# Moving the past keys' norms of a hybrid encoder step into its S5 phase, with a changed formula for them

## The chip, the cores and the metric

One core of a Trainium2 chip runs the whole program. The metric is device microseconds (us) of one execution. The kernel before took 1456.39 us, the median of 3 runs (1454.52 to 1458.11).

## The reference

One step of a two-layer encoder, over 512 prompt tokens and 32 sample tokens that go through together (544 columns). Layer 0 has an S5 branch (a diagonal complex recurrence with a GLU gate) beside an attention into 256 memory tokens. Layer 1 has latent attention: a shared latent of 256 features gives the keys and values of 12 heads. The sample tokens also attend to 1024 cached positions, whose latents are an input. For these the keys have to be normed, head by head:

```python
m = rms_norm(mem[None], mem_norm_g[:, None, None, :])
kv = jnp.einsum('lbmd,ldk->lbmk', m, w_mem_kv)
...
latent_all = jnp.concatenate([past_latent.astype(new_latent.dtype), new_latent], axis=1)
...
k_nope = rms_norm((latent_all @ w_uk).reshape(Bsz, Lk, MLA_HEADS, NOPE_DIM), k_nope_norm_g)
```

The kernel needs only the sums of squares of those cached keys (64 features for each of 12 heads and 1024 positions); the scores themselves are taken with the query pulled through `w_uk`, and multiplied by the inverse norm afterwards. The two layers end in gated feed-forward blocks that take most of the time.

## The kernel before

Everything is float32 at almost full precision: an operand is split into a high part rounded to `float32r` and a low part, the rest, and a product takes three matmuls (high by high, high by low, low by high; `combos`). A weight is loaded twice: once plainly by SP's queue into `wraw`, from which ScalarE (ACT) writes the high part and the negated high part, and once by an accumulating transfer from GpSimd's (POOL's) queue, which adds the weight onto the negated high part and so leaves the low part (`weights`, L227 to L235). Everything else with a gain or a norm is split by ACT (high) and VectorE (DVE, low).

The program is written as stages and generators. A framework sorts the instructions of each engine beforehand, by the order of writing and by the table `ORDER`: a unit with a positive number is put earlier by so many places, one with a negative number later. At run time each engine, SP's and POOL's queues among them, works its list strictly in order, so an instruction that waits holds back all behind it. PSUM's eight banks and the pools of SBUF slots (`F`, `R`, `WR`, `WH`, `WL`) are taken and given back in the order of writing.

Two places matter here.

*The S5 phase* (67 to 174 us) has six steps `m`. A step transposes its inputs (`s5_input`), makes weights on DVE (`s5_wv`, `s5_wc`), writes a small kernel to DRAM and reads it back in another layout (the tile `kp` gets its diagonal added by POOL at L707, L710 writes it to `kd`, L719 reads it), scans on DVE (`s5_scan`, L752 to L780), multiplies out (`s5_output`, L791 and L792, transposes at L803) and applies GELU. Between the steps `fill` puts units of `mem_kv`: eight that project 256 memory rows by a quarter of the features of one layer (matmuls at L350; the rows are multiplied by the gain and split by ACT at L344 and DVE at L345), then nine that take norms, transposes and outputs. By `fills` seven of the first eight are written into steps 0 to 4, the eighth into step 5, and seven of the nine behind the last step. Then comes the memory attention of layer 0 (`mem_attend`, L430 to L520) and the GLU product (a GEMM like all others, matmuls at L324).

*The query phase* of layer 1 (742 to 866 us) has, in this order of writing: latents of the new tokens (L1197 to L1248), three groups of queries in turn, `q_front(g)` (a projection, L1289 and L1308) and `q_back(g)` (norm and rotation on DVE and POOL, L1298 to L1339, transposes at L1345 and L1351), beside them `key_norms`, then `absorb` (L1364 to L1375) and `sample_scores` (L1423). `key_norms` has three groups of four heads. For each it splits the group's part of `w_uk`, and for each of nine tiles of positions (eight of the past, 128 each, and one of 32 new ones) it multiplies six times (L1395: positions on the partitions, 256 columns), squares on ACT (L1399) and sums by head on DVE (L1401). `rsqrt` of the whole table `kss` follows. `load_past` loads the past latents and splits them; `sample_scores` needs them too.

Of the kernel before, what the change touches and what calls it, by code (L numbers as in the profile page):

```python
# [18 lines left out]
KD = D // 128  # L19
# [31 lines left out]
for _n, _w in (("mix", 2 * KD), ("bglu", NM), ("ffn", 2 * KD), ("kv", KD), ("mem", 2 * KD), ("ql", NM),  # L51
# [8 lines left out]
NCN = 468  # L60


ORDER = {"q_front": -50, "q_back": -20, "absorb": -100, "mem_kv": -60, "mem_kv_end": 580, "s5_scan": 400,
         "s5_input": 260, "norm0": 20, "s5_params": -50, "mem_attend0": 100, "s5_wc": 10, "q_front0": 10, "norm1": 0,
         "att1": 30, "att2": 20, "mem_attend1": 20, "load_past": -100, "queries": 10, "key_norms": 60,
         "latents": 1250, "queries2": -160}
# [71 lines left out]
def body(ctx, tc, A, O):  # L138
# [67 lines left out]
    def gcol(name, i):  # L206
        c = GP[name] + i
        return gp[:, c:c + 1]
# [125 lines left out]
    def mem_kv(fm, rm, bm, b1, dst):  # L334
        ps = [[bm.get(512) for _ in range(2)] for _ in range(2)]
        acc = fm.get(2, NMEM)
        for u in range(4):
            mt = fm.get(2, NMEM)
            nc.sync.dma_start(mt, A["mem"][:, 2 * u:2 * u + 2, :])
            for l in range(2):  # L340
                hi, lo = rm.get(2, NMEM), rm.get(2, NMEM)
                for k2 in range(2):
                    g = gcol("mem", l * KD + 2 * u + k2)
                    S.activation(hi[:, k2], mt[:, k2], AF.Copy, scale=g)  # L344
                    V.scalar_tensor_tensor(lo[:, k2], mt[:, k2], g, hi[:, k2].bitcast(F32), ALU.mult, ALU.subtract)  # L345
                w = weights(A["w_mkv"][l, u], 1024, lo_eng=V if l else P)
                for t in range(2):
                    for k2 in range(2):
                        for i, (x, ww) in enumerate(combos((hi, lo), w)):
                            T.matmul(ps[l][t], x[:, k2, 128 * t:128 * t + 128], ww[:, 512 * k2:512 * k2 + 512],  # L350
                                     start=u == 0 and k2 == 0 and i == 0, stop=u == 3 and k2 == 1 and i == 2)
                wfree(w)
                rm.put(hi, lo)
                if l:
                    if u:
                        q = fm.get(2, NMEM)
                        S.activation(q, mt, AF.Square)
                        P.tensor_tensor(acc, acc, q, ALU.add)
                        fm.put(q)
                    else:  # L360
                        S.activation(acc, mt, AF.Square)
                    fm.put(mt)
                yield
# [10 lines left out]
        for l in range(2):  # L374
            kt, v = dst[l]
            ss = sm(8, "mss")
            q = fm.get(2, 256)
            for t in range(2):
                S.activation(q[:, t], ps[l][t][:, :256], AF.Square, scale=r[:, t:t + 1])
                S.activation(v[:, t, :], ps[l][t][:, 256:], AF.Copy, scale=r[:, t:t + 1])  # L380
            V.tensor_reduce(ss, view(q, [[64, 8], [1, 64]]), AX.X, ALU.add)
            P.dma_start(O["mem_v"][l].rearrange("t p c -> p t c"), v)
            yield
            x = sm(8, "mkx")
            V.tensor_scalar(x, ss, 1.0 / 64, EPS, ALU.mult, ALU.add)
            y = rsqrt(x, 128, 8, "mkr")
            fm.put(q)
            V.tensor_tensor(y.rearrange("p (t h) -> p t h", t=2), y.rearrange("p (t h) -> p t h", t=2),
                            view(r, [[1, 2], [0, 4]]), ALU.mult)
            yield  # L390
            kk = fm.get(2, 256)
            for t in range(2):
                V.tensor_tensor(kk[:, t].rearrange("p (h d) -> p h d", d=64),
                                ps[l][t][:, :256].rearrange("p (h d) -> p h d", d=64),
                                view(y, [[1, 4], [0, 64]], 4 * t), ALU.mult)
            bm.put(*ps[l])
            kf = view(kk, [[64, 8], [1, 64]])
            V.tensor_tensor(kf, kf, view(grow(f"mk{l}"), [[0, 8], [1, 64]]), ALU.mult)
            P.dma_start(O["mem_k"][l].rearrange("t p c -> p t c"), kk)
            yield  # L400
            pt = b1.get(512)
            for hp in range(2):
                for t in range(2):
                    T.transpose(pt[:, 256 * hp + 128 * t:256 * hp + 128 * t + 128],
                                kk[:, t, 128 * hp:128 * hp + 128], ident)
            S.activation(kt.rearrange("p a b -> p (a b)"), pt, AF.Copy, scale=mqg[:, l:l + 1])
            b1.put(pt)
            fm.put(kk)
            yield

    def mem_cache(l, fm):
        kt, v, raw = fm.get(2, NMEM), fm.get(2, 256), fm.get(2, NMEM)
# [588 lines left out]
    exr.close()  # L1001
    exr = ExitStack()
    lr = exr.enter_context(tc.tile_pool(name="l0b", bufs=1, reuse_waits="tile"))
    R, fx = slots(lr, 4, F32R, 512, "rb"), slots(lr, 3, F32, FW, "fx")
    FA, FB, FD = slots(lr, 2, F32, 1024, "wv"), slots(lr, 1, F32, 2 * FW, "tb"), slots(lr, 3, F32, 2 * FW, "wc")
    fxs = list(fx.free)
    F.merge(fx)
# [1 line left out]
    kvp = F.get(2, NMEM), F.get(2, 256)  # L1009
    mkv = mem_kv(F, R, BG, BS, (kvp, (mk1, mv1)))  # L1010

    fills = ((1, 2, 1), (1, 1, 0), (1, 0, 0), (0, 1, 0), (1, 1, 0), (1, 1, 0), (7,))
    nfill = 0

    def fill(n):
        nonlocal nfill
        for _ in range(n):
            unit("mem_kv" if nfill < 8 else "mem_kv_end", mkv)
            nfill += 1
    wvs = []  # L1020

# [43 lines left out]
    while unit("s5_output_end", g_out) is not g_out:  # L1065
        pass
    fill(20)
    P.dma_start(O["ssm"], q5["hf"])
    F.retire(big, *fxs)
    exr.close()  # L1070
# [305 lines left out]


    def key_norms():
        ss = sm(108, "kss", 1)
        tc.keep_in_program_order(V.memset(ss, 1.0))  # L1380
        for g in range(3):
            raw, w = F.get(2, 256), (R.get(2, 256), R.get(2, 256))
            nc.sync.dma_start(raw, A["w_ukv"][g][:, :, :256])
            split(*w, raw)
            F.put(raw)
            for tp in range(5):
                b = BK.get(512)
                n = NS if tp == 4 else 128
                for j in range(1 if tp == 4 else 2):
                    t = 2 * tp + j  # L1390
                    for k in range(2):
                        x = lat[k] if tp == 4 else past[t // 4][k]
                        c0 = 512 if tp == 4 else 128 * (t % 4)
                        for c, (xx, ww) in enumerate(combos(x, w)):
                            T.matmul(b[:n, 256 * j:256 * j + 256], xx[:, c0:c0 + n], ww[:, k], start=k == 0 and c == 0,  # L1395
                                     stop=k == 1 and c == 2)
                q = F.get(512)
                m = 256 if tp == 4 else 512
                S.activation(q[:n, :m], b[:n, :m], AF.Square)  # L1399
                BK.put(b)  # L1400
                V.tensor_reduce(view(ss[:n], [[12, m // 256], [1, 4]], 24 * tp + 4 * g),  # L1401
                                q[:n, :m].rearrange("p (j h d) -> p j h d", h=4, d=64), AX.X, ALU.add)
                F.put(q)
                if tp % 2:
                    yield
            R.put(*w)
            yield
        x = sm(108, "kx", 1)
        V.tensor_scalar(x, ss, 1.0 / NOPE, EPS, ALU.mult, ALU.add)
        res["rk"] = rsqrt(x, 128, 108, "krs")  # L1410


# [388 lines left out]
```

## Time and profile before

| | us |
|---|---|
| median of 3 runs | 1456.39 |
| lowest, highest | 1454.52, 1458.11 |
| profiled execution, its own time | 1456.27 |
| its span, first to last instruction | 1454.5 |
| PE busy | 1407.3 (97%) |
| ACT busy | 754.4 (52%) |
| DVE busy | 721.8 (50%) |
| POOL busy | 358.5 (25%) |

The profiled execution lies 0.12 us from the median, and 1.8 us of it are outside the span. Busy shares are means over stages with different limits: the feed-forward blocks keep PE (TensorE) at work without a break, and only the S5 phase, the start and a few places in layer 1 show it idle. The page's line of the granted clock (PEclk, tenths of full speed) has a dip in the same places. A time read in the trace is counted from the span's start.

### The profile page before, as it was taken

What the parts mean: (1) busy time and instruction counts of PE and PEld (TensorE: products, weight loads), DVE (VectorE), ACT (ScalarE), POOL (GpSimd) and SP (SyncE); (2) the same over time, 40 slices, a digit from 0 to 9 for tenths busy, and PEclk for the clock granted to TensorE, in tenths of its full rate; (3) what the DMA queues carried; (4) which work ended last, traced back from release to release, by engine and by line L of the source; (5) the groups of instructions that cost most, each with busy time, mean ns of one, the idle gap of its engine ahead of it and who ended that gap; (6) DMA issues with size and microseconds to landing.
All of it is one profiled execution on the core that took longest, in us unless ns stands there. A gap on an engine that the chain in (4) does not pass through costs nothing.

```text
span 1454.5 us, 26917 instructions
## 1 busy us (share of the span) xinstructions
PE 1407.3 (97%) x10693; PEld 1314.2 (90%) x10693; DVE 721.8 (50%) x1810; ACT 754.4 (52%) x1247; POOL 358.5 (25%) x622
## 2 busy tenths in 40 slices
PE   8977799999999999999989999999999999999998
PEld 7966689999999999999988987557999999999998
DVE  7988742355513551455247755663355513551351
ACT  6655655555534553456554554654555534553452
POOL 2131232312211221124326422332322211221121
PEclk9989889999999999999999999999999999999999
DMA  8754627778878878869741432012778888878775
GB/s 264 167 139 111 165 59 176 164 173 176 177 173 175 175 174 175 175 143 205 151 124 58 108 112 54 19 30 52 160 174 177 172 176 175 179 170 179 172 159 138
DMA packets 71902, 214.77 MB, mean 148 GB/s; under 512 B 8128, under 2 KB 17312, under 8 KB 71776
## 3 DMA queue, kind: packets, MB, share of 16 engines
q0 software_dynamic: 27616, 96.16, 37.4%
q1 hardware_dynamic: 43008, 114.80, 27.4%
q10 hardware_dynamic: 1152, 2.10, 0.5%
q8 instruction: 84, 1.38, 0.4%
q14 instruction: 42, 0.34, 0.1%
HBM read 207.41 MB, written 5.61 MB: 146 GB/s over the span
## 4 chain that ended last, share of the span: by engine, by line
PE 86%; DVE 4%; DMA 4%; ACT 3%; issue 2%; POOL 1%; SPq 0%; DVEq 0%; POOLq 0%; ACTq 0%
PE bank L324 66%; PE bank L1308 2%; PE bank L1556 2%; PE bank L1395 2%; PE bank L1592 1%; DMA wlo<-i_w_in 1%; PE bank L1509 1%; PE bank L1483 1%; PE bank L1197 1%; DMA wlo<-i_w_f 1%; PE bank L350 1%; PE bank L1581 1%; PE bank L482 1%; PE bank L520 1%; PE bank L1423 1%
## 5 line engine op out<-in xcount | busy, mean ns | idle before, releaser
L324 PE MATMUL bank<-rc,whi 128*128 128x272 f32 x3728 | 628.3, 289 | 0.2 <-DVE rc L305 0.2
L324 PEld LDWEIGHTS bank<-rc,whi 128*128 128x128 f32 x3728 | 529.7, 189 | 5.2 <-issue 4.3
L324 PE MATMUL bank<-rc,wlo 128*128 128x272 f32 x1864 | 389.0, 289 | 0.8 <-DMA wlo<-i_w_in 0.8
L231 ACT ACTIVATE whi<-wraw 128x1024 fp32r<-128x1024 f32 (+2 forms) x186 | 191.2, 1028 | 361.0 <-issue 314.4
L324 PEld LDWEIGHTS bank<-rc,wlo 128*128 128x128 f32 x1864 | 293.7, 188 | 1.3 <-DMA wlo<-i_w_in 1.0
L324 PE MATMUL bank<-g,whi 128*128 128x272 f32 x1408 | 234.6, 288 | 0.7 <-ACT g L216 0.7
L324 PEld LDWEIGHTS bank<-g,whi 128*128 128x128 f32 x1408 | 198.8, 188 | 1.3 <-ACT g L216 1.2
L233 POOL DMA_DIRECT2D wlo<-i_w_f x136 | 117.4, 863 | 304.1 <-ACT wlo L232 302.2
L232 ACT ACTIVATE wlo<-wraw 128x1024 fp32r<-128x1024 f32 (+2 forms) x186 | 188.9, 1016 | 3.7 <-PE bank L350 3.1
L324 PE MATMUL bank<-g,wlo 128*128 128x272 f32 x704 | 145.9, 289 | 2.4 <-DMA wlo<-i_w_f 2.4
L851 DVE SCALAR_TENSOR_TENSOR fa<-fa,gp,fa 128x546 f32<-128x546 f32 x88 | 69.6, 791 | 139.7 <-ACT fa L850 139.7
L865 DVE TENSOR_TENSOR h<-bank,h 128x272 f32<-128x272 f32 x96 | 38.2, 435 | 173.0 <-PE bank L324 172.5
L324 PEld LDWEIGHTS bank<-g,wlo 128*128 128x128 f32 x704 | 110.4, 188 | 2.8 <-DMA wlo<-i_w_f 2.8
L850 ACT ACTIVATE fa<-fa,gp 128x546 f32<-128x546 f32 x88 | 73.1, 830 | 12.8 <-DVE fa L845 12.8
L843 DVE TENSOR_TENSOR fa<-bank,fa 128x272 f32<-128x272 f32 x88 | 38.9, 442 | 81.8 <-PE bank L324 77.6
L852 DVE SCALAR_TENSOR_TENSOR fa<-fa,gp,fa 128x546 f32<-128x546 f32 x88 | 69.6, 790 | 3.1
L891 ACT ACTIVATE fa<-fa 128x546 f32<-128x546 f32 x44 | 29.1, 662 | 71.8 <-DVE fa L852 71.8
L847 POOL COPY fa<-gp 128x2 f32<-128x2 f32 x88 | 20.9, 238 | 171.5 <-DVE g L217 108.0
L848 POOL COPY fa<-fa 128x4 f32<-128x4 f32 x88 | 18.0, 205 | 166.0 <-DVE fa L845 166.0
L324 PE MATMUL bank<-ra,whi 128*128 128x272 f32 x256 | 48.1, 311 | 2.3 <-ACT whi L241 2.3
L216 ACT ACTIVATE g<-fa 128x544 fp32r<-128x544 f32 x44 | 29.0, 658 | 37.6 <-DVE fa L893 37.6
L892 DVE TENSOR_TENSOR fa<-fa,fa 128x512 f32<-128x512 f32 x44 | 30.5, 693 | 33.5 <-ACT fa L891 33.5
(626 smaller groups left out, 1992.7 us busy)
## 6 DMA issues: line engine op xcount, KB each, us to landing
wraw<-i_w_f SPq DMA_DIRECT2D x120, 512.0 KB
wlo<-i_w_f POOLq DMA_DIRECT2D x120, 512.0 KB, 7.4
wraw<-i_w_out SPq DMA_DIRECT2D x16, 512.0 KB
wlo<-i_w_out POOLq DMA_DIRECT2D x16, 512.0 KB, 7.2
wraw<-i_w_in SPq DMA_DIRECT2D x14, 512.0 KB
wlo<-i_w_in POOLq DMA_DIRECT2D x14, 512.0 KB, 7.8
wraw<-i_w_f SPq DMA_DIRECT2D x16, 384.0 KB
wlo<-i_w_f POOLq DMA_DIRECT2D x16, 384.0 KB, 6.3
```

Of the source, the lines that this page charges most:

```text
L231: S.activation(hi, raw, AF.Copy)
L232: S.activation(lo, raw, AF.Copy, scale=-1.0)
L233: P.dma_start(lo, ap, accum_op=ALU.add)
L324: T.matmul(ps[q][:, :c], ww, xx[:, c0:c0 + c], start=k == 0 and i == 0, stop=k == n - 1 and i == 2)
L843: V.tensor_tensor(u[:, 2:274], ps[0][:, :272], rb[:, :272], ALU.mult)
L850: S.activation(y, u[:, 2:548], AF.Identity, scale=gcol("cw", 3 * ci + 2), bias=gcol("cb", ci))
L851: V.scalar_tensor_tensor(y, u[:, 1:547], gcol("cw", 3 * ci + 1), y, ALU.mult, ALU.add)
L852: V.scalar_tensor_tensor(y, u[:, 0:546], gcol("cw", 3 * ci), y, ALU.mult, ALU.add)
L865: V.tensor_tensor(h[m][:, c0:c0 + cc], ps[qd][:, :cc], h[m][:, c0:c0 + cc], ALU.add)
L891: S.activation(yg, yg, AF.Silu)
L892: V.tensor_tensor(u[:, 2:514], ya[:, :NP], yg[:, :NP], ALU.mult)
L1308: T.matmul(b[:, :384], xx[:, 128 * t:128 * t + 128], ww[:, 384 * (k % 2):384 * (k % 2) + 384], start=k == 0 and i == 0, stop=k == NM - 1 a ...
```

## The change

Three things change together.

1. The past keys' norms leave `key_norms` and become a generator `past_norms`, twelve units, put into the S5 steps. It works with features on the partitions: for each half of the positions (512) and each pair of heads, six matmuls of 512 columns with the weight as the stationary operand (L440), one square on ACT (L442), and four small float32 matmuls against `blk2` that sum 64 partitions each (L446) into a bank, which ACT copies into `kss` at the end of each half (L451). Latents and weights are loaded by SP's queue (L421, L430) and split as weights are: two ACT passes and an accumulating transfer from POOL's queue (L424, L433). The weights are loaded once for each half. `key_norms` keeps the 32 new positions alone. The past latents are still loaded and split in the query phase.
2. In `mem_kv` the multiplied rows are made by POOL (L343), the high and negated high part by ACT in passes of 512 columns, and the low part by an accumulating transfer from SBUF to SBUF (L346). DVE has no part in it.
3. `fills` puts all 17 units of `mem_kv` into steps 0 to 3, ten units of `past_norms` into steps 4 and 5 and two behind the last. `mem_kv_end` goes from 580 to 60. The pool `R` of the phase grows from 4 to 8 tiles, `fx` shrinks from 3 to 2.

```diff
-"mem_kv_end": 580
+"mem_kv_end": 60
...
             for l in range(2):
-                hi, lo = rm.get(2, NMEM), rm.get(2, NMEM)
+                hi, lo, gm = rm.get(2, NMEM), rm.get(2, NMEM), fm.get(2, NMEM)
                 for k2 in range(2):
-                    g = gcol("mem", l * KD + 2 * u + k2)
-                    S.activation(hi[:, k2], mt[:, k2], AF.Copy, scale=g)
-                    V.scalar_tensor_tensor(lo[:, k2], mt[:, k2], g, hi[:, k2].bitcast(F32), ALU.mult, ALU.subtract)
+                    P.tensor_scalar(gm[:, k2], mt[:, k2], gcol("mem", l * KD + 2 * u + k2), 0.0, ALU.mult, ALU.add)
+                S.activation(hi, gm, AF.Copy)
+                S.activation(lo, gm, AF.Copy, scale=-1.0)
+                P.dma_start(lo, gm, accum_op=ALU.add)
+                fm.put(gm)
...
+    def past_norms(fm, rm, bm, ss):
+        for hf_ in range(2):
+            c = slice(512 * hf_, 512 * hf_ + 512)
+            st = bm.get(512)
+            xs = []
+            for i in range(2):
+                raw, hi, lo = fm.get(512), rm.get(512), rm.get(512)
+                nc.sync.dma_start(raw, A["lat_past"][:, i, c])
+                S.activation(hi, raw, AF.Copy)
+                S.activation(lo, raw, AF.Copy, scale=-1.0)
+                P.dma_start(lo, A["lat_past"][:, i, c], accum_op=ALU.add)
+                fm.put(raw)
+                xs.append((hi, lo))
+            for g in range(3):
+                raw, wh, wl = fm.get(2, 256), rm.get(2, 256), rm.get(2, 256)
+                ap = A["w_ukv"][g][:, :, :256]
+                nc.sync.dma_start(raw, ap)
+                S.activation(wh, raw, AF.Copy)
+                S.activation(wl, raw, AF.Copy, scale=-1.0)
+                P.dma_start(wl, ap, accum_op=ALU.add)
+                fm.put(raw)
+                for j in range(2):
+                    b = bm.get(512)
+                    f = slice(128 * j, 128 * j + 128)
+                    for k in range(2):
+                        for i, (x, w) in enumerate(combos(xs[k], (wh[:, k, f], wl[:, k, f]))):
+                            T.matmul(b, w, x, start=k == 0 and i == 0, stop=k == 1 and i == 2)
+                    q = fm.get(512)
+                    S.activation(q, b, AF.Square)
+                    bm.put(b)
+                    for t in range(4):
+                        o = 12 * t + 4 * g + 2 * j
+                        T.matmul(st[:, o:o + 2], q[:, 128 * t:128 * t + 128], blk2, start=True, stop=True)
+                    fm.put(q)
+                    if j:
+                        rm.put(wh, wl)
+                    yield
+            S.activation(ss[:, 48 * hf_:48 * hf_ + 48], st[:, :48], AF.Copy)
...
-    fills = ((1, 2, 1), (1, 1, 0), (1, 0, 0), (0, 1, 0), (1, 1, 0), (1, 1, 0), (7,))
+    fills = ((2, 0, 0), (1, 1, 1), (1, 1, 1), (3, 4, 2), (2, 2, 1), (2, 2, 1), (2,))
...
     def key_norms():
...
-            for tp in range(5):
-                b = BK.get(512)
-                n = NS if tp == 4 else 128
...
+            b = BK.get(512)
+            for k in range(2):
+                for c, (xx, ww) in enumerate(combos(lat[k], w)):
+                    T.matmul(b[:NS, :256], xx[:, 512:512 + NS], ww[:, k], start=k == 0 and c == 0,
+                             stop=k == 1 and c == 2)
```

How the lists move is seen at three places. Line numbers are those of each kernel; the changed one has 44 lines more in front of the S5 helpers and some 50 in front of the query phase.

PE in the query phase, behind the second group's transposes (L1345 and L1351 before, L1395 and L1401 now). Before, `absorb` of groups 0 and 1 (L1364) is followed by 54 matmuls of `key_norms` (L1395; the first rows are shown):

```order
L1345 MATMUL bank_70<-cn,fa_91 96x128
L1351 MATMUL bank_63<-cn,fa_77 96x128
L1364 MATMUL bank_68<-qsT_6897,wraw_94 128x32 x8
L1364 MATMUL bank_64<-qsT_6898,wraw_95 128x32 x8
L1395 MATMUL bank_65<-rc_1895,rc_1885 128x256
```

Now, from the same point, absorb is L1414, and directly behind it stand the third group's 16 transposes (L1395), then its own absorb and the scores (L1463):

```order
L1395 MATMUL bank_70<-cn,fa_78 96x128
L1401 MATMUL bank_63<-cn,fa_86 96x128
L1414 MATMUL bank_68<-qsT_7083,wraw_94 128x32 x8
L1414 MATMUL bank_66<-qsT_7084,wraw_95 128x32 x8
L1395 MATMUL bank_64<-cn,fa_92 96x128
```

The 96 past matmuls of groups 1 and 2 that stood between the two sets of transposes, or among the second set, are gone, and nothing has taken their place.

PE between the last transposes of the S5 output (L803 before, L847 now) and the GLU product (L324). Before, the memory keys' transposes (L404) and the start of the memory attention (L430 to L482) stand there:

```order
L803 MATMUL bank_70<-cn,big 128x69 x4
L449 MATMUL bank_69<-fa_79,fa_73 128x256 x2
L404 MATMUL bank_68<-cn,fx_853 128x128 x4
L430 MATMUL bank_68<-cn,fa_71 128x2 x4
L430 MATMUL bank_68<-cn,fa_74 128x2 x4
L439 MATMUL bank_68<-cn,fa_76 128x1 x2
```

Now 30 of the 72 matmuls L440 and 7 of the 12 sets of L446 stand there, with the start of the memory attention (L474 to L526); the end of that stretch:

```order
L446 MATMUL bank_67<-cn,big 128x2 x4
L440 MATMUL bank_66<-rb_854,rb_849 128x512
L526 MATMUL bank_64<-fa_89,fa_87 128x256
L526 MATMUL bank_65<-fa_89,fa_87 128x256
L446 MATMUL bank_67<-cn,fa_76 128x2 x4
L526 MATMUL bank_64<-fa_89,fa_87 128x256
L526 MATMUL bank_65<-fa_89,fa_87 128x256
L474 MATMUL bank_68<-cn,fa_76 128x2 x4
L483 MATMUL bank_68<-cn,fa_91 128x1 x2
L324 MATMUL bank_66<-rc_2067,whi_98 128x272
```

The memory keys' transposes have moved ahead, into the S5 steps, and the past keys stand in their room.

POOL around the last two additions to `kp` (L707 before, L751 now). Before, one weight transfer stands between POOL's small work for the scans and the last addition:

```order
L782 COPY hf<-big 128x16
L759 MEMSET fx_853 128x8
L233 DMA wlo_99<-i_w_mkv 128x1024
L358 TENSOR_TENSOR fx_855<-fx_855,fa_79 128x512
L233 DMA wlo_100<-i_w_glu 128x768
L707 TENSOR_TENSOR kp<-kp,big 128x2x16
```

Now four transfers of `past_norms` (L424, L433) stand between the last two additions:

```order
L751 TENSOR_TENSOR kp<-kp,fa_77 128x2x16
L424 DMA rb_852<-i_lat_past 128x512
L826 COPY hf<-fa_74 128x16
L433 DMA rb_854<-i_w_ukv 128x2x256
L801 MEMSET big 128x8x2
L803 MEMSET fa_76 128x8
L433 DMA rb_856<-i_w_ukv 128x2x256
L433 DMA rb_854<-i_w_ukv 128x2x256
L749 TENSOR_TENSOR fx_858<-cn,sp_145 128x32
L751 TENSOR_TENSOR kp<-kp,fx_858 128x2x16
```

The last addition, which starts the round trip of `kd` for step 5, now stands behind a transfer that writes `rb_854` a second time, and so behind the matmuls that read it the first time.

## Rows read from the trace of the kernel before

**Rows 1.** The page's first part: busy us, share of the span, instructions.

```profile
span 1454.5 us, 26917 instructions
PE 1407.3 (97%) x10693; PEld 1314.2 (90%) x10693; DVE 721.8 (50%) x1810; ACT 754.4 (52%) x1247; POOL 358.5 (25%) x622
```

**Rows 2.** Busy by stretch: us; PE, PEld, DVE, ACT, POOL; clock; DMA share, GB/s.

```profile
67.00:174.00 107.00, 84.41 (x762) 69.58 (x760) 89.56 (x181) 65.31 (x149) 27.06 (x43) 0.90 0.56 136
174.00:188.00 14.00, 11.39 (x40) 8.41 (x40) 6.42 (x26) 3.33 (x9) 2.46 (x4) 0.53 0.44 114
775.00:842.00 67.00, 66.63 (x490) 61.76 (x479) 46.36 (x129) 35.12 (x73) 31.47 (x53) 0.95 0.38 104
```

**Rows 3.** Chain that ended last, 774 to 846 us: start, us, piece.

```profile
774.58 0.80 PE bank L1289 x32
775.38 0.32 PE bank L1395
...
794.89 2.85 PE bank L1395 x24
...
815.73 1.75 PE bank L1345 x16
...
817.72 4.83 PE bank L1364 x32
822.55 8.51 PE bank L1395 x54
839.51 1.91 PE bank L1364 x16
...
841.78 4.27 PE bank L1423 x23
```

**Rows 4.** Busy by stretch, two us of the query phase, columns as in rows 2.

```profile
820.00:822.00 2.00, 2.00 (x12) 2.00 (x11) 1.68 (x6) 1.20 (x3) 0.74 (x2) 0.51 0.68 203
```

**Rows 5.** Timeline of DVE and POOL: start, us, line, operation, what ended idle time.

```profile
816.67 0.55 DVE L1298 TENSOR_REDUCE qss<-fe 128x12 f32<-128x384 f32 x1 [2.55 <-ACT fe L1297]
...
821.26 1.38 POOL L1335 TENSOR_TENSOR fa<-fa,qrs 128x128 f32<-128x128 f32 x2 [9.63 <-ACT rc L216]
...
827.70 0.34 POOL L1339 TENSOR_TENSOR fa<-fa 128x64 f32<-128x64 f32 x1
```

**Rows 6.** Chain that ended last, 172 to 192 us, behind the S5 steps.

```profile
173.06 0.74 PE bank L803 x8
...
179.51 3.58 PE bank L430 x16
...
188.13 3.92 PE bank L324 x16
```

**Rows 7.** Chain in layer 1, 886 to 896 us: prices of matmuls at full clock.

```profile
890.40 0.93 PE bank L1509 x4
891.33 0.79 PE bank L430 x8
```

**Rows 8.** Timeline of ACT and POOL: prices for 512 and 256 columns.

```profile
149.15 0.59 ACT L683 ACTIVATE fa<-bank 128x512 f32<-128x512 f32 x1
...
212.71 2.00 POOL L498 TENSOR_SCALAR fa<-fa,zri 128x256 f32<-128x256 f32 x4 [0.18 <-DVE zri L495]
```

**Rows 9.** The page's DMA issues: count, KB each, median us to landing.

```profile
wlo<-i_w_f POOLq DMA_DIRECT2D x16, 384.0 KB, 6.3
```

**Rows 10.** One line's instructions by form: ns min/median/max, first and last start.

```profile
L345 DVE SCALAR_TENSOR_TENSOR rb<-fa,gp,rb x12: 461/478/1499, 96.1 to 160.5; 128x256 fp32r<-128x256 f32 x12
```

**Rows 11.** Timeline of all engines, two overlapping operations of POOL and DVE.

```profile
150.74 2.64 POOL L358 TENSOR_TENSOR fx<-fx,fa 128x512 f32<-128x512 f32 x1 [0.31 <-ACT fa L357]
...
152.17 1.50 DVE L345 SCALAR_TENSOR_TENSOR rb<-fa,gp,rb 128x256 fp32r<-128x256 f32 x1
```

**Rows 12.** Timeline of PE, the first output matmuls of the last S5 step.

```profile
164.64 0.69 PE L791 MATMUL bank<-fa,fa 128*69 128x128 f32 x2 [2.45 <-DMA fa<-kd]
```

**Rows 13.** Timeline of POOL: an issue of an accumulating transfer.

```profile
154.00 0.88 POOL L233 DMA_DIRECT2D wlo<-i_w_glu  x1 [0.62 <-ACT wlo L232]
```

More of the change, by code (lines that the diff above doesn't have):

```diff
@@ L60 @@
 NCN = 468
-ORDER = {"q_front": -50, "q_back": -20, "absorb": -100, "mem_kv": -60, "mem_kv_end": 580, "s5_scan": 400,
+ORDER = {"q_front": -50, "q_back": -20, "absorb": -100, "mem_kv": -60, "mem_kv_end": 60, "s5_scan": 400,
          "s5_input": 260, "norm0": 20, "s5_params": -50, "mem_attend0": 100, "s5_wc": 10, "q_front0": 10, "norm1": 0,
@@ L409, in mem_kv @@
             yield
+    def past_norms(fm, rm, bm, ss):
[36 more added lines that the diff above has]
+            S.activation(ss[:, 48 * hf_:48 * hf_ + 48], st[:, :48], AF.Copy)
+            bm.put(st)
+            free2(rm, xs)
     def mem_cache(l, fm):
@@ L1003, in body @@
     lr = exr.enter_context(tc.tile_pool(name="l0b", bufs=1, reuse_waits="tile"))
-    R, fx = slots(lr, 4, F32R, 512, "rb"), slots(lr, 3, F32, FW, "fx")
+    R, fx = slots(lr, 8, F32R, 512, "rb"), slots(lr, 2, F32, FW, "fx")
     FA, FB, FD = slots(lr, 2, F32, 1024, "wv"), slots(lr, 1, F32, 2 * FW, "tb"), slots(lr, 3, F32, 2 * FW, "wc")
@@ L1010, in body @@
     mkv = mem_kv(F, R, BG, BS, (kvp, (mk1, mv1)))
-    fills = ((1, 2, 1), (1, 1, 0), (1, 0, 0), (0, 1, 0), (1, 1, 0), (1, 1, 0), (7,))
+    kss = sm(108, "kss", 1)
+    pnm = past_norms(F, R, BG, kss)
+    fills = ((2, 0, 0), (1, 1, 1), (1, 1, 1), (3, 4, 2), (2, 2, 1), (2, 2, 1), (2,))
     nfill = 0
@@ L1017, in fill @@
         for _ in range(n):
-            unit("mem_kv" if nfill < 8 else "mem_kv_end", mkv)
+            if nfill < 17:
+                unit("mem_kv" if nfill < 8 else "mem_kv_end", mkv)
+            else:
+                unit("past_norms", pnm)
             nfill += 1
@@ L1067, in body @@
     fill(20)
+    assert nfill > 31
     P.dma_start(O["ssm"], q5["hf"])
@@ L1378, in key_norms @@
     def key_norms():
-        ss = sm(108, "kss", 1)
-        tc.keep_in_program_order(V.memset(ss, 1.0))
+        tc.keep_in_program_order(V.memset(kss[:, 96:], 1.0))
         for g in range(3):
@@ L1385, in key_norms @@
             F.put(raw)
-            for tp in range(5):
-                b = BK.get(512)
-                n = NS if tp == 4 else 128
[L1389 to L1405, printed above, removed]
+            b = BK.get(512)
[3 more added lines that the diff above has]
+                             stop=k == 1 and c == 2)
+            q = F.get(256)
+            S.activation(q[:NS], b[:NS, :256], AF.Square)
+            BK.put(b)
+            V.tensor_reduce(kss[:NS, 96 + 4 * g:100 + 4 * g], q[:NS].rearrange("p (h d) -> p h d", d=64), AX.X,
+                            ALU.add)
+            F.put(q)
             R.put(*w)
@@ L1408, in key_norms @@
         x = sm(108, "kx", 1)
-        V.tensor_scalar(x, ss, 1.0 / NOPE, EPS, ALU.mult, ALU.add)
+        V.tensor_scalar(x, kss, 1.0 / NOPE, EPS, ALU.mult, ALU.add)
         res["rk"] = rsqrt(x, 128, 108, "krs")
```

## The prediction

> **What bounds the kernel now.** I read the page's first part to see who works all the time: PE is busy for 1407.3 of 1454.5 us, ACT and DVE for half of it [rows 1]. On that mean alone, the removed matmuls are a gain and the added ones a loss, one for one. The change touches two stages only, so the busy time by stretch comes next [rows 2]. In the S5 phase (67 to 174 us) PE is busy for 84.4 of 107 us, DVE for 89.6, ACT for 65.3, POOL for 27.1: no engine is full, DVE is nearest, and PE has 22.6 us of holes. Behind the last step (174 to 188) PE is busy for 11.4 of 14 us, but at a granted clock of 0.53. In the query phase (775 to 842) PE is busy for 66.6 of 67 us: whatever leaves PE's list there is worth its own time, until something else becomes the last wait. The chain of waits says so too: from 774 to 842 it is made of PE's pieces [rows 3]. So the question is whether the work finds room in the S5 phase, and how much of what leaves the query phase is real.
>
> **Query phase.** 144 of the 162 matmuls L1395 go (three groups, eight tiles of past positions, six each); 18 for the new positions stay. The piece of 24 took 2.85 us, 0.119 us each [rows 3], so all 144 at that price are 17.1 us, the ceiling as far as PE's list goes. 48 of them stand ahead of 815.73. At 0.119 these are 5.7 us. But ten run in alternation with small ones, one L1395 taking 0.32 and the two L1289 beside it about as much, while 32 L1289 alone take 0.80, or 0.025 each: an alternating turn returns some 0.55 us, which makes the ceiling for the 48 about 10 us. The new positions' matmuls still alternate with something. I take 8 us. PE then ends the absorb of groups 0 and 1 (L1364 x32, 822.55 before) at about 814.5.
>
> There the cover ends. The 54 L1395 (8.51 us) that followed hid the third group's norm and rotation. Its projection ended at 815.6 before, the reduction on DVE started at 816.67, POOL's products at 821.26 and the last one ended at 828.04 [rows 5]: a chain of 12.4 us, of which the change removes nothing (four 0.7 us sums by head on DVE leave it at best). With the projection 8 us earlier, at 807.6, the transposes can go on at about 820. PE waits some 5.5 us, a wait that was not there. Then come 16 transposes (1.75), 6 L1438 (0.7), and absorb with its eviction (839.51 to 841.78, 2.27): scores at 824.7 if the clock stays full, 17 us earlier. It need not stay full: from 820 to 822 PE was busy all the time at a granted clock of 0.51, that is 1.2 GHz, behind a quieter stretch [rows 4]. At that clock transposes, L1438 and absorb cost 4.4 us more, and scores start at 829.1, 12.7 us earlier; some of the first scores at the low clock take a little more. I take **-12 us**, bounds -9 and -15. DVE's and ACT's relief there (24 sums, 12 squares) is hidden under PE already and counted at nothing.
>
> **S5 phase, what is added on PE.** 72 L440 of 512 columns at 0.23 (four took 0.93) are 16.8 us, and 48 small float32 L446 at 0.1 to 0.2 (eight records, four matmuls, took 0.79) are 4.8 to 9.5 [rows 7]. By the order 42 L440 and 20 L446 stand in steps 4 and 5, about 13 us, into 22.6 us of holes [rows 2]; but the holes of the two last steps are a third of that. Bounds 0 (all in holes) and 13; I take +4, since PE's wait for the next step's data [rows 12] is not longer for being filled, but the work written into a step does sit ahead of the next one.
>
> The other 30 L440 and 28 L446 stand behind the last step: 7.0 and 2.8 to 5.6 us. What stood there are the memory keys' transposes, now earlier, and the memory attention, together from 173.8 to 188.13 with PE half idle in its chain (16 L430 took 3.58 us there at the low clock, against 0.79 for 8 at full [rows 6, 7]). The attention's chain of DVE and ACT stays, some 10 us, and the past keys run inside it; at full clock I get 14.3 to 16.5 us of PE work for a stretch that took 14.3. The GLU's first matmul (L324) starts 2 us later: **+2**, bounds -4 and +6.
>
> **ACT, POOL and DVE there.** ACT gets ten pairs of splits and twelve squares of 512 columns at 0.59 [rows 8], 19 us, and the wider passes of `mem_kv` 2 more, into 41.7 us of holes: bounds 0 and 21, I take +2, because ACT's list is where inputs of a step queue behind fills. DVE loses 16 L345 at 0.478, 7.6 us [rows 10]. It is the fullest engine of the steps, but often stands in the chain for other reasons; I take -2, bounds 0 and -7.6. POOL gets 16 multiplications of 256 columns at 0.50 [rows 8], 8 us, and 18 more issues of transfers at 0.88 [rows 13], 16 us, into 80 us of holes: nothing by itself. Each accumulating transfer lands up to 6.3 us after its issue [rows 9] (384 KB; these are at most 256 KB), which lengthens the way from memory rows to L350; covered by the units being written a step ahead. Where it shows is the rival A. SP's ten added loads, of at most 256 KB, go into a stretch in which the transfers' engines are busy for 0.55 of the time [rows 2], and cost nothing.
>
> **Sum.** S5 phase +4 +2 +2 -2 = +6, query phase -12: 6 us off the profiled execution's 1456.27, 1450. That execution lies 0.12 us below the median of the runs.
>
> **Rivals.**
>
> A, slower: POOL's list. `kd`'s round trip is already the last wait of the last step: PE stood 2.45 us for it [rows 12]. In the new order the last addition to `kp`, which starts that trip, stands behind a transfer that rewrites `rb_854`, which waits for twelve L440 that wait for the first transfers. One such turn is 0.88 of issue, 6.3 to land, 2.8 of matmuls, 1.2 of two ACT passes: 11.2 us; the slots of `R` taken over from `mem_kv` can make it two. The matmuls then fill the hole they make, so the +4 falls away: -10 and a delay of 14 to 22 us give 1460 to 1469, middle 1464. It decides from a delay of 14 us. For it: POOL works strictly in order. Against: the units are written in front of the addition, and could run while DVE, not POOL, is late. One turn alone gives 1457.5, no change. Chance 0.23 (for two), 0.06 (for one).
>
> B, no change: DVE and POOL stand in each other's way. L345 has a median of 0.478 us and a maximum of 1.499 [rows 10]; that one ran from 152.17 to 153.67, while POOL's addition L358 ran until 153.38, 0.29 before [rows 11]. If every one of the 16 new multiplications stops a DVE operation so for its whole 0.5 us, 8 us come back for the 7.6 that left: the -2 becomes up to +5.5, and the sum 1457. Against: 1.499 is the longest of 12, and the median shows nothing of it. The Trainium skill has a rule for that: in "SBUF — State Buffer", section "SBUF: two separate sides", a DVE operation with two SBUF inputs and a GpSimd operation that reads SBUF share a port pair by an exclusive lock, and the other "fully blocks". The row of 1.50 us agrees with it. Chance 0.08.
>
> C, the S5 phase takes it all: holes take the matmuls, and the tail, which was at half clock, is no longer than before: S5 +0 to -2, sum 1443. For it: 22.6 us of holes; against: the fills' ACT work. Chance 0.2.
>
> D, the query phase returns only what stood before the third transposes, 5.7, and the new idle costs clock: -8 and +6, 1454, no change. Chance 0.08.
>
> **How the numbers follow.** The forecast keeps 0.35, with 1447 to 1452. About 0.3%, 4.4 us, is what a measurement of this kernel tells from no change. Faster: forecast and C, 0.55. The same: one turn of A, B and D, 0.22. Slower: A, 0.23. The range goes from 1440 (C with the query phase's bound of -15) to 1466, which leaves out the upper part of A.
>
> **What would show it.** In the changed profile: the scores (L1463) start 12 to 15 us earlier relative to the GLU's start, with an idle PE of about 5 us before the third set of transposes, and a low granted clock behind it. The GLU's L324 starts at 192 to 196 instead of 188.1. The stretch from 174 on has a higher clock than 0.53. If instead L324 starts beyond 200 and the output matmuls of the last step (L835) wait for `kd` for ten or more us, it is A; if L324 starts at or ahead of 188, it is C; if DVE's operations in steps 0 to 3 have grown by 0.5 us each beside L343, it is B. The forecast is wrong in its base if PE does not wait before the third transposes: then the chain I measured is not what limits it.

## The result and the profile after

The changed kernel takes 1507.18 us (median of 4 runs, 1505.1 to 1518.52) beside 1457.09 us for the kernel before: ratio 1.0364, interval 1.0337 to 1.0392. It is 50 us slower, where 6 us less were forecast, and 41 us beyond the top of the range. The lines of the page that answer to [rows 1]:

```profile
span 1503.2 us, 27049 instructions
PE 1429.9 (95%) x10717; PEld 1327.1 (88%) x10717; DVE 709.9 (47%) x1782; ACT 767.7 (51%) x1269; POOL 384.1 (26%) x656
```

PE's busy time grew by 22.6 us, the span by 48.7: half of the loss is waiting. Where it arises is read from a mark that both kernels have, the eight small matmuls L260 behind the GLU product and its layer's sums, in the chain of waits; first before, then after, with the chain of the scores behind it:

```profile
287.30 0.78 PE bank L260 x8
```

```profile
344.73 0.79 PE bank L260 x8
...
869.83 1.75 PE bank L1395 x16
...
888.04 11.26 PE bank L1463 x54
```

At the mark the changed kernel is 57.4 us late. From the mark to the scores it takes 543.3 us, before 554.5 [rows 3]; the end comes 48.7 us late, so all that follows the mark returns 8.7. The S5 phase cost 57 where I had 6, and the query phase returned 9 where I had 12.

The S5 phase's pace is read from POOL's timeline at the additions to `kp`, one per step. Before (steps 3, 4 and 5):

```profile
119.78 1.55 POOL L707 TENSOR_TENSOR kp<-kp,fa 128x32 f32<-128x32 f32 x1 [1.85 <-issue]
...
141.58 0.25 POOL L707 TENSOR_TENSOR kp<-kp,fa 128x32 f32<-128x32 f32 x1 [7.30 <-ACT kp L706]
...
156.23 0.24 POOL L707 TENSOR_TENSOR kp<-kp,big 128x32 f32<-128x32 f32 x1 [1.35 <-issue]
```

After, the same three, and what stands ahead of the last:

```profile
146.02 1.34 POOL L751 TENSOR_TENSOR kp<-kp,big 128x32 f32<-128x32 f32 x1
...
180.23 0.51 POOL L751 TENSOR_TENSOR kp<-kp,fa 128x32 f32<-128x32 f32 x1 [3.40 <-issue]
...
194.21 1.10 POOL L433 DMA_DIRECT2D rb<-i_w_ukv  x1 [5.13 <-ACT rb L432]
200.61 1.06 POOL L433 DMA_DIRECT2D rb<-i_w_ukv  x1 [5.30 <-ACT rb L432]
205.62 0.23 POOL L749 TENSOR_TENSOR fx<-cn,sp 128x32 f32<-128x32 f32 x1 [3.95 <-PE bank L446]
205.93 0.25 POOL L751 TENSOR_TENSOR kp<-kp,fx 128x32 f32<-128x32 f32 x1
```

Step 3 is 26.2 us late, before any past unit has run (their first instruction is a load at 156.5); step 4 is 38.6 late, step 5 49.7. What was late in between, in the chain of the changed kernel:

```profile
118.10 6.52 DMA rb<-fa
...
128.53 7.45 DMA fx<-i_mem
...
148.33 3.35 DMA rb<-fa
...
155.64 7.15 DMA wraw<-i_w_glu
...
186.16 5.49 DMA rb<-i_w_ukv
191.69 3.61 PE bank L440 x9
195.31 5.28 issue
200.61 1.06 POOL rb L433
201.67 3.90 issue
```

The transfer of the memory rows' low part (`rb<-fa`, L346) and the load of the rows stand in the chain with their whole landing time. Then it goes from a weight's transfer to PE, to ACT's splits of the next weight, to POOL, and to a slot that L446 has to give back for L749. SP is held too, from 157 to 179 us, by a store of the memory keys whose slot the second load of past latents wants:

```profile
SPq L421 <- DMA o_mem_k<-fx: 22.0, 1, 22.0
```

Busy time by stretch after, columns as in [rows 2]; the last two stretches are the last step and what follows it, up to L324 at 243.9 (188.13 before [rows 6]):

```profile
175.00:191.00 16.00, 11.28 (x90) 8.97 (x90) 6.42 (x13) 9.13 (x23) 3.92 (x8) 0.79 0.56 142
191.00:222.00 31.00, 26.77 (x199) 22.38 (x200) 9.56 (x21) 15.34 (x34) 6.99 (x11) 0.89 0.59 140
222.00:244.00 22.00, 21.70 (x129) 18.05 (x129) 1.90 (x4) 8.93 (x20) 2.06 (x3) 0.91 0.21 37
```

PE is full behind 222 and nearly so behind 191. So two readings were open: PE's added work (P), or loads, splits and transfers in series, with PE full only because it works late and at a lower clock (W).

### The profile page after: what moved, and what is told of

Its sections match the earlier page's. It is cut to its first block, busy times and chain, and to the rows that moved or that the text cites. A ratio compares the mean times of both kernels' runs of the same rounds, so it can differ in the third digit from the quotient of the medians.

```text
span 1503.2 us, 27049 instructions
## 1 busy us (share of the span) xinstructions
PE 1429.9 (95%) x10717; PEld 1327.1 (88%) x10717; DVE 709.9 (47%) x1782; ACT 767.7 (51%) x1269; POOL 384.1 (26%) x656
## 4 chain that ended last, share of the span: by engine, by line
PE 77%; DMA 5%; DVE 4%; issue 3%; ACT 3%; POOL 2%; SPq 1%; DVEq 0%; POOLq 0%; ACTq 0%
PE bank L324 61%; PE bank L1596 2%; PE bank L1358 2%; PE bank L1632 1%; PE bank L1549 1%; DMA fa<-kd 1%; PE bank L1523 1%; DMA wlo<-i_w_f 1%; PE bank L1621 1%; PE bank L1247 1%; PE bank L440 1%; PE bank L1463 1%; PE bank L352 1%; PE bank L564 1%; DMA rb<-fa 1%
## 5 line engine op out<-in xcount | busy, mean ns | idle before, releaser
L324 PE MATMUL bank<-rc,whi 128*128 128x272 f32 x3728 | 626.7, 289 | 0.3 <-DVE rc L305 0.2
L324 PEld LDWEIGHTS bank<-rc,whi 128*128 128x128 f32 x3728 | 527.9, 188 | 4.5 <-issue 3.1
L324 PE MATMUL bank<-rc,wlo 128*128 128x272 f32 x1864 | 388.1, 288 | 0.3 <-DMA wlo<-i_w_in 0.3
L324 PEld LDWEIGHTS bank<-rc,wlo 128*128 128x128 f32 x1864 | 292.4, 188 | 1.9 <-issue 1.3
L324 PE MATMUL bank<-g,whi 128*128 128x272 f32 x1408 | 235.7, 289 | 0.8 <-ACT g L216 0.8
L324 PEld LDWEIGHTS bank<-g,whi 128*128 128x128 f32 x1408 | 200.1, 189 | 1.4 <-ACT g L216 1.2
L324 PE MATMUL bank<-g,wlo 128*128 128x272 f32 x704 | 146.5, 290 | 2.7 <-DMA wlo<-i_w_f 2.7
L324 PEld LDWEIGHTS bank<-g,wlo 128*128 128x128 f32 x704 | 111.0, 189 | 3.1 <-DMA wlo<-i_w_f 3.1
L324 PE MATMUL bank<-ra,whi 128*128 128x272 f32 x256 | 47.6, 308 | 3.1 <-ACT whi L241 3.1
```

The costliest lines, as they stand in the source:

```text
L324: T.matmul(ps[q][:, :c], ww, xx[:, c0:c0 + c], start=k == 0 and i == 0, stop=k == n - 1 and i == 2)
```

## The experiments

All times are medians; for the slower kernels the intervals of the ratios reach 2 to 7 us to either side.

**Without past norms, S5 phase as before.** In `key_norms` the matmuls of the change alone; the table of sums is filled with ones:

```diff
-            for tp in range(5):
...
+            for k in range(2):
+                for c, (xx, ww) in enumerate(combos(lat[k], w)):
```

> Kernel before, with the past keys' norms left out altogether (their part of the table is set to one): S5 phase as before, query phase as after. In the changed kernel the scores start 9.5 us earlier against the GLU's start than before, and the end comes 7.1 us earlier against it. If that is the query phase's own gain, 1457 - 7 = 1450 (1447 to 1452). If the query phase's gain was 12 us or more and the changed kernel lost some of it to work pushed on from the S5 phase, 1445 or less. If the past matmuls were only cover, 1455 to 1459.

Measured: 1450.53, ratio 0.9964 (0.9949 to 0.9978), so 5.6 us. This is all that any removal of the past norms in this order can bring. The chain and then PE's timeline of this run show why it isn't 12:

```profile
803.75 11.90 PE bank L1308 x59
815.65 1.75 PE bank L1345 x16
...
833.86 11.24 PE bank L1414 x54
```

```profile
791.02 0.31 PE L1389 MATMUL bank<-rc,rc 128*32 128x256 f32 x1 [1.49 <-ACT rc L216]
...
802.97 0.78 PE L1389 MATMUL bank<-rc,rc 128*32 128x256 f32 x5 [0.92 <-DVE rc L217]
824.55 0.66 PE L1345 MATMUL bank<-cn,fa 128*96 128x128 f32 x2 [2.82 <-DVE fa L1339]
825.99 0.45 PE L1345 MATMUL bank<-cn,fa 128*96 128x128 f32 x1 [0.78 <-POOL fa L1339]
827.49 1.73 PE L1345 MATMUL bank<-cn,fa 128*96 128x128 f32 x7 [1.05 <-POOL fa L1339]
```

The third projection ends at 815.65, where it ended before (815.73 [rows 3]). From 774 to 816 PE is busy for 38.1 us instead of 42.0: the 3.9 us between are waits for split weights of the new positions, as in the rows at 791 and 803. The granted clock of that stretch is 0.96 instead of 1.00, and its first small matmuls start 0.9 us later. Ahead of the third transposes it waits 4.65 us, near the 5.5 forecast. The scores start 7.9 us earlier, and their first 54 matmuls take 11.24 instead of 9.68.

**Memory rows alone.** The rows' low parts and the slots of the change in the kernel before:

```diff
-                    V.scalar_tensor_tensor(lo[:, k2], mt[:, k2], g, hi[:, k2].bitcast(F32), ALU.mult, ALU.subtract)
+                P.dma_start(lo, gm, accum_op=ALU.add)
```

> Kernel before with only the memory rows' low parts changed (POOL multiplies, two ACT passes, accumulating transfer) and the slots of the change; fills, order and past norms as before. Theory 1 (the detour of POOL and the transfer holds back the matmuls on the memory rows and with them the steps): slower by 15 to 26 us, 1472 to 1483, the delay that the fourth addition to kp shows in the changed kernel (146.0 against 119.8). Theory 2 (the detour is covered when units are written where they were, the new fills do the harm): within 5 us of before.

Measured: 1459.11, ratio 1.0016 (0.9992 to 1.0039). Alone, in the old places, the detour costs nothing that can be told from no change. Theory 1 falls as it stood.

**Fills alone.**

```diff
-    fills = ((1, 2, 1), (1, 1, 0), (1, 0, 0), (0, 1, 0), (1, 1, 0), (1, 1, 0), (7,))
+    fills = ((2, 0, 0), (1, 1, 1), (1, 1, 1), (3, 4, 2), (0, 0, 0), (0, 0, 0), (0,))
```

> Kernel before with only the 17 units of the memory keys written into steps 0 to 3 as the change does (and 60 for their last nine), rows split as before, past norms in the query phase as before. Theory 2 (new fills): slower by 15 to 26 us. Theory 1 (the detour): within 5 us, or faster by up to 8, since the memory keys' transposes leave the stretch behind the last step.

Measured: 1461.35, ratio 1.0039 (1.0022 to 1.0056), 5.2 us. That is at the edge of what theory 1 allowed and far from theory 2: it costs a little, though the stretch behind the last step is emptied. Its chain goes over DVE in step 3, where the units' small work stands.

**Change with the old rows.**

```diff
-                P.dma_start(lo, gm, accum_op=ALU.add)
+                    V.scalar_tensor_tensor(lo[:, k2], mt[:, k2], g, hi[:, k2].bitcast(F32), ALU.mult, ALU.subtract)
```

> The changed kernel with the memory rows split as before, by ACT and DVE. Theory 1: the 15 to 26 us of steps 0 to 3 come back, 1481 to 1492. Theory 2: 1505 to 1509, and the fourth addition to kp still near 146. If past norms alone do the harm, it stays at 1507 with the delay moved into steps 4 and 5.

Measured: 1496.95, ratio 1.0278 (1.0249 to 1.0308): 10 us back, less than theory 1 had; the fourth addition to `kp` comes at 130.4 instead of 146.0. In the dense places of steps 0 to 3 the detour does cost, by the transfers in the chain above; where units stand apart (the run with the rows alone) it doesn't. Most of the loss is elsewhere.

**Change without past units.** `past_norms` is not called, the fills of steps 4, 5 and behind are empty.

```diff
+    fills = ((2, 0, 0), (1, 1, 1), (1, 1, 1), (3, 4, 2), (0, 0, 0), (0, 0, 0), (0,))
```

> The changed kernel without the past units (their part of the table is set to one, so the result of the sample tokens' scores is not the reference's); memory rows and the first 17 fills as changed. Both theories of the past units (P: their PE work, 35 us by the trace; W: the waits they bring into POOL's and SP's lists and the slots) say that what is left is memory rows and fills alone: 1458 to 1466, that is the 5 us of the fills and the 3 us of the rows on top of 1450.5. If those two do more together than apart (the fourth addition to kp is 26 us late in the changed kernel, and all of it is paid), 1475.

Measured: 1465.35, ratio 1.0054 (1.0036 to 1.0072). So of the 56.7 us between the change (1507.18) and the S5 phase of before with no past norms (1450.53), the past units carry 41.8, rows and fills together 14.8.

This run also shows that a late addition to `kp` is not yet a loss. The fourth and fifth come at 144.2 and 178.0 here, almost as late as in the changed kernel (146.0 and 180.2). The sixth comes 9 us behind the fifth, and the mark L260 is reached at 299.25, 12 us behind before: units that are written earlier leave a shorter stretch later.

**Past units split by DVE.**

```diff
-                S.activation(wl, raw, AF.Copy, scale=-1.0)
-                P.dma_start(wl, ap, accum_op=ALU.add)
+                split(wh, wl, raw)
```

> The changed kernel with the low parts of the past units made by DVE's subtraction instead of a negated pass and an accumulating transfer: ten ACT passes and ten issues of POOL fewer, ten DVE operations of 512 columns more. W (POOL's list, rival A): POOL's 5.3 us waits for L432 and the landings go, the last addition to kp comes 8 to 14 us earlier and the time falls to 1485 to 1497. P (PE work): 1503 to 1511.

Measured: 1495.32, ratio 1.0247 (1.022 to 1.0273): 12 us back, the time that W had, but not in the way it had: the last addition to `kp` comes at 205.0, 0.9 us earlier and not 8 to 14, L324 4.5 us earlier (239.4 instead of 243.9), and the profile ends 8.1 us earlier. So the shorter turn (no landing, one pass of ACT less) is worth about 12 us by the medians; that it is POOL's list ahead of `kp` that it relieves is not shown.

**A third of the past units' matmuls, all of their loads.**

```diff
-                        for i, (x, w) in enumerate(combos(xs[k], (wh[:, k, f], wl[:, k, f]))):
-                            T.matmul(b, w, x, start=k == 0 and i == 0, stop=k == 1 and i == 2)
+                        x, w = (xs[0][0], wl[:, 0, f]) if k == 0 else (xs[1][1], wh[:, 1, f])
+                        T.matmul(b, w, x, start=k == 0, stop=k == 1)
...
-                    for t in range(4):
+                    for t in range(1):
```

> The changed kernel with all loads, splits, transfers and squares of the past units, but two of the six L440 of a unit and one of its four L446 (the past keys' sums are wrong then): 48 of 72 and 36 of 48 go. In the changed kernel these took 23.3 and 11.7 us of PE (0.32 and 0.24 each), so 24 us of PE leave and every wait for a transfer, a slot or a queue stays. P: 1483 (1480 to 1490). W: 1500 to 1508.

Measured: 1501.1, ratio 1.029 (1.0258 to 1.0322). 6 us, not 24: P as the only limit falls. Behind the last addition to `kp` (202.47) the chain of this run goes over loads, splits and transfers of the past units up to L324:

```profile
203.66 6.25 DMA fa<-i_w_ukv
...
210.60 4.51 DMA fa<-i_lat_past
...
220.19 4.31 DMA rb<-i_w_ukv
...
234.19 5.21 PE bank L324 x22
```

From the last addition to L324 it takes 31.7 us instead of 38.0, and the addition itself comes 3.5 us earlier; 5.7 of these 9.7 us are left at the end of the profile. The last stretch in front of L324, columns as before, shows where the rest went:

```profile
222.00:234.20 12.20, 9.66 (x32) 6.83 (x32) 1.42 (x2) 2.52 (x6) 0.00 (x0) 0.51 0.22 43
```

PE is busy for 9.7 of 12.2 us with 32 records of matmuls, at a granted clock of 0.51 (1.2 GHz); in the changed kernel it had 129 records in 22 us, at 0.91. Ahead of it, from 205 to 222, PE is busy for 11.6 us instead of 13.5. With fewer matmuls PE waits more, and what is left runs slower: that PE was full there was no proof that PE alone set the time.

**All past units behind the S5 steps**, rows and memory units as before (the slots stay those of the change).

```diff
-    fills = ((2, 0, 0), (1, 1, 1), (1, 1, 1), (3, 4, 2), (2, 2, 1), (2, 2, 1), (2,))
+    fills = ((1, 2, 1), (1, 1, 0), (1, 0, 0), (0, 1, 0), (1, 1, 0), (1, 1, 0), (5,))
```

> Memory rows and memory units as before, all past units behind them, most of them behind the last step, so that kp is not behind them. P: the S5 steps are as before, and 35 us of PE less the 7 us that the stretch behind the last step had to spare at full clock, less 6 to 9 for the query phase: 1474 to 1480. W: with the last addition to kp free, most of the loss goes: below 1465.

Measured: 1498.99, ratio 1.0261 (1.0229 to 1.0293). Neither: 48 us above the run without past norms, though `kp` is not behind them (its last addition comes at 159.2, 3 us later than before). W in the form "they hold back kp" falls too. The chain of this run, one of its shorter executions (span 1489.9):

```profile
182.63 9.33 issue
191.98 5.56 DMA rb<-i_w_ukv
...
204.86 4.31 DMA rb<-i_w_ukv
209.22 4.21 PE bank L438 x9
```

Here too the units wait for their own loads and transfers one after another, up to 209. From there to 233 the chain lies on PE: it is busy for 37.6 of the 40 us from 200 to 240, at a granted clock of 0.74. So both limits show in one stretch, one behind the other.

**One turn.** One load and split of the latents and of one weight group; all units use these.

```diff
-            for i in range(2):
+            for i in range(2 if hf_ == 0 else 0):
...
-                raw, wh, wl = fm.get(2, 256), rm.get(2, 256), rm.get(2, 256)
+                if w is None:
+                    raw, wh, wl = fm.get(2, 256), rm.get(2, 256), rm.get(2, 256)
```

> The changed kernel with all matmuls, squares and sums of the past units, but one load and split of two latent tiles and of one weight group instead of ten of the kind (all units use the first ones, so the past keys' sums are wrong). Waits in series as the only limit: 1467 to 1475. Two limits side by side, PE's 26 us at full clock being the other: 1485 to 1495. PE alone: 1503 to 1508.

**One turn and a third of the matmuls.** Both edits together.

> Both at once: the past units with one load and split of latents and of weights instead of ten pairs (all units use the first ones), and a third of the matmuls as in the run with a third of PE's work. (The past keys' sums are wrong.) If loads, splits and transfers in series are one limit and PE's work another of about the same length, removing both returns far more than the sum of the two alone: 1466 to 1480, near the 1465 without past units. If there is a third thing (slots, squares, the place in the lists), it stays above 1490.

Measured: one turn 1492.39 (ratio 1.0252, 1.0202 to 1.0301), both 1476.85 (1.0137, 1.0108 to 1.0165). Less PE work alone brings 6.1 us, fewer turns alone 14.8, both 30.3. Each theory of one limit is out, and both times lie where two limits side by side had them. With turns gone, the same cut of PE work brings 15.5 instead of 6.1; but with these intervals the surplus of 9 us of both over the sum is not certain by the times alone. What speaks for it is the chain of loads and transfers in the run with a third of the matmuls, beside the full PE of the run with one turn. The busy time by stretch of the run with one turn shows that with the turns gone PE is the limit, and at full clock:

```profile
191.00:205.00 14.00, 14.00 (x108) 11.52 (x106) 6.95 (x14) 4.08 (x7) 2.40 (x4) 1.00 0.09 29
205.00:222.00 17.00, 17.00 (x135) 15.59 (x134) 1.92 (x6) 7.21 (x18) 0.31 (x1) 1.00 0.21 57
```

Of the past units' 41.8 us, 11.5 are left then, for one turn, squares and a third of the matmuls; this rest wasn't taken apart. The run with both edits has a candidate for it in its chain: the store of the memory keys (`o_mem_k<-fx`, landed at 178.75), and behind it the load of past latents that waits for its slot. SP stands for that store for 24.3 us there, and for 22.0 in the changed kernel, in which the pool `fx` has one slot less than before. No run takes this wait out, so its share is open; the run with all units behind the steps doesn't have it and loses 48 us all the same.

**Norms of the new positions later**, in the kernel without past norms.

```diff
-"key_norms": 60
+"key_norms": -200
```

> The kernel without any past norms (query phase of the change, S5 phase as before, 1450.5) with the new positions' matmuls put 260 places later in the order. Theory: the query phase returned 6 instead of 12 because these 18 matmuls, whose weights are loaded and split late, now stand bare in front of the projections of groups 1 and 2 (PE waited from 784 to 803 for norms' weights and small work of DVE), where the past matmuls used to fill that time. Then the third group's projection ends earlier than 815.7 and the time falls by 4 to 8 us, 1443 to 1447. If DVE's and POOL's chains set that time, it stays within 2 us.

Measured: 1446.78, ratio 0.9931 (0.9909 to 0.9952). The time came out as expected, about 4 us below, with intervals that just overlap; the reason is not shown. In the profile of this run, its longest execution (span 1450.4), the third projection ends at 816.00:

```profile
810.81 5.19 PE bank L1308 x28
...
836.45 11.05 PE bank L1414 x54
```

Counted from the mark L260, at 289.86 here and at 287.05 without the move, the projection ends 2.5 us earlier, but the scores start only 0.2 us earlier. The chain ahead of 810 goes over POOL's issues of weights and outputs and DVE's norms in place of the new positions' weights. So it stays open what sets the third projection's end once these are out of its way.

**Kernel before, past matmuls earlier.**

```diff
-"key_norms": 60
+"key_norms": 110
```

> The kernel before with one number changed, key_norms from 60 to 110: the past matmuls of the first group stand in one block of 24 in front of the second group's small matmuls instead of alternating with them, and more of the rest stand ahead of the third group's transposes. What a version without any past norms saves is 6 us, so that is the ceiling. If the alternation (0.6 us a turn) is a price of its own, 1451 to 1454; if it is only time in which PE would wait anyway, within 3 us of before.

Measured: 1454.04, ratio 0.998 (0.9966 to 0.9994), 17 runs of before beside it: a small gain, and the only version here with all of the computation that beats both kernels. Its chain:

```profile
774.57 2.83 PE bank L1395 x24
777.40 1.13 PE bank L1289 x48
...
811.20 1.75 PE bank L1345 x16
...
838.84 9.73 PE bank L1423 x54
```

The block of 24 costs 2.83, and the 48 small matmuls behind it 1.13, where each alternating turn took about 0.6 [rows 3]. The third projection ends 4.5 us earlier, the scores start 2.9 earlier. The time alone doesn't decide between the two: 1454.04 lies at the upper end of the one range and within 3 us of before (1456.6) too. The rows do: PE is busy without a gap in both kernels from 774.5 to 784.5, at a granted clock of 1.00, so the alternation had a price of its own and was not time in which PE would have waited.

## Why the prediction was wrong, point by point

**Query phase: right in sign, too large.** The step that failed is "with the projection 8 us earlier". Without past norms it ended at 815.65, not 807.6; in the changed kernel it ended 3.3 us earlier, counted from the mark L260. I had summed what leaves PE's list and not asked what the matmuls that stay, with weights loaded and split late, would wait for: these waits are 3.9 of the 8 us, the clock and the later start a part of the rest. The 10 us from which I took the 8 were high too: of the past matmuls eight alternate with small ones and not ten, which makes it 9.2 at the same prices. The wait for the third group was right (4.65 us against 5.5), and so was the low clock behind it. In the changed kernel:

```profile
872.00:886.00 14.00, 8.68 (x52) 7.27 (x51) 8.42 (x30) 7.15 (x16) 6.18 (x15) 0.63 0.53 169
```

8.7 us in that profile, 5.6 by the runs without past norms, in place of 12.

**S5 phase: the holes.** The step that failed worst is "about 13 us, into 22.6 us of holes", +4: with the +2 behind the steps the sum had 6 us for the past units, and they cost 41.8. A hole in PE's time is a time in which PE's next data is on its way, and the past units bring data of their own, on the same lists, in turns: load, two passes of ACT, issue, landing, matmuls. I priced one such turn, 11.2 us, in rival A, and then only ahead of the last `kp`. There are ten pairs of splits; the slots of `R` let few of them overlap. The run with all of them behind the steps costs 48 us without touching `kp`. Rival A named the mechanism, the place and the direction (1464 at 0.23), but let it end at `kp`. Of its two signs one came: L324 started beyond 200 (243.9), but the last step's L835 waited for `kd` for 2.9 us in all and not for ten.

**PE's added work: a little undersized.** By the busy time of their lines in the changed kernel, the 72 L440 take 23.3 us (0.32 each against 0.23) and the 48 L446 11.7 (0.24 each against 0.1 to 0.2): 35 in place of 21.6 to 26.3. But busy times of lines that follow each other overlap, and the clock was 0.88 there from 185 to 244. In the run with one turn, with PE full at a clock of 1.00, the six and the four of a unit (L442 and L448 there) start like this:

```profile
198.93 1.64 PE L442 MATMUL bank<-rb,rb 128*128 128x512 f32 x6
200.40 0.98 PE L448 MATMUL bank<-cn,fa 128*128 128x2 f32 x8
201.24 1.64 PE L442 MATMUL bank<-rb,rb 128*128 128x512 f32 x6
```

A unit takes 2.31 us, twelve of them 27.7. That is little above the upper end of what I had; the larger part of the miss lies in the waits, and in the clock that goes with them.

**Behind the last step: +2.** It is 38 us from the last addition to `kp` to L324 (205.93 to 243.9), 32 before (156.23 to 188.13 [rows 6]), although the memory keys had left. The clock did rise, as forecast (0.91); the work was larger than the room.

**Rows and fills: "covered by the units being written a step ahead".** They were not: with all eight projecting units written into steps 0 to 2 (before, seven of them in steps 0 to 4 and one in step 5), the landing of L346 stands in the chain, at 118.10 and 148.33. Rows and fills cost 14.8 us together, 3 and 5 alone.

**Rival B** was seen, small, and the other way round. The multiplications in the first and the last of the four forms:

```profile
L343 POOL TENSOR_SCALAR big<-big,gp x4: 470/1281/2278, 66.3 to 69.4; 128x256 f32<-128x256 f32 x4
...
L343 POOL TENSOR_SCALAR fa<-fx,gp x4: 470/474/1564, 136.2 to 144.5; 128x256 f32<-128x256 f32 x4
```

It was POOL that was stretched, by up to 1.8 us an operation. Of DVE's operations from 60 to 150 us the products of L716 grew from 0.68 us before to 0.88, 1.7 us for nine; no other large group grew by more than 0.06 an operation, where B's sign was 0.5 us each. The Trainium skill ("SBUF — State Buffer", section "SBUF: two separate sides") has the one that starts second blocked; no run here took the port apart from the rest. **C** and **D** are out: the phase took nothing for free, and the query phase returned 5.6, near what D had for it (5.7 to 8), beside a loss that D didn't have.

## What to carry to other kernels

Idle time of an engine is room only for work whose operands are already there: before moving work into it, count the turns of load, split, issue and landing that it brings, and how many of them the slots let overlap. Leave the work out altogether as the first experiment: here that gave 5.6 us, a ceiling that no place for the work could have beaten in that order. And where independent matmuls stand in an order made by numbers, look for rows that alternate with small ones: one number returned half of that ceiling at no other cost.

## What was not expected of the hardware

With two thirds of the past units' matmuls left out, PE was still busy for 9.7 of the last 12.2 us in front of the GLU product, with 32 records, since the granted clock there was 0.51; with all of them it was busy for 21.7 of 22 us, with 129 records, at 0.91. And a square sum by a matmul of two float32 columns took 0.21 us in the run with one turn, at full clock (eight records from 198.08 to 198.93 are four of them), not much less than one of 512 columns in the rounded format (0.25).
